# Output projection of a transformer block: the seventh product's weights are added onto the third's tiles in place

## The chip, the cores and the metric

One core of one Trainium2 chip runs the whole kernel. The metric is device time in microseconds of one execution; for each kernel it is the median of several runs. The profile is one execution recorded by the hardware profiler.

## What is computed

A block with adaptive layer norm, a mixer of a short convolution and sparse attention, an output projection and a gated FFN, on 512 tokens of width 2048, everything in float32. The change is in the output projection, whose place is:

```
y_conv = short_conv_mixer(cb, cc, ch, conv_w)          # 512 x 1024, then a norm
y_attn = nsa_mixer(q, kc, vc, ksl, vsl, kw, vw, gl..)  # 512 x 1024, then a norm
x = x + g_a * (concat([y_conv, y_attn]) @ w_out)       # w_out: 2048 x 2048
h = modulate(rms_norm(x, norm_ffn), sh_f, sc_f)
x = x + g_f * ((silu(h @ ffn_w1) * (h @ ffn_w3)) @ ffn_w2)
```

## The kernel before, in words

TensorE multiplies float32 matrices as three products of rounded parts: every operand is split into a high part (ScalarE casts it to fp32r, tiles `whi`) and a low part (VectorE subtracts the high part from the source, `wlo`).

The projection is cut into 2 x 2 x 2 blocks of 256 tokens, 1024 rows and 1024 columns of `w_out`, and is done with seven block products in place of eight (a Strassen-Winograd scheme). A product is named by its number p, in the order 2, 1, 5, 6 and 3 interleaved, 7, 4. Its weights are eight blocks j = 0 to 7 of 128 x 1024 floats (512 KB), so that (p, j) is one unit of work: a load or an addition of weights, a split of the block (`y_split`, L1216 to L1234), and twelve matmuls of 128 x 512 (`y_mm`, L1242). The 56 units are numbered in the list `yu`: product 2 is 0 to 7, product 1 is 8 to 15, product 5 is 16 to 23, products 6 and 3 share 24 to 39, product 7 is 40 to 47, product 4 is 48 to 55. Units 36 to 41 are (6,6), (6,7), (3,6), (3,7), (7,0) and (7,1). Of product 7 the last two units, of product 4 the last three are multiplied together.

The weights of products 1, 5, 6 and 4 lie in eight tiles `wt` and are made one out of the other: B11 is loaded, B12 added (product 5), B22 added (product 6), B21 added (product 4). Product 3's weights are B22 as it is, and VectorE adds the same tiles onto `wt` for product 6 (L1446). Product 7's weights are B12 + B22. Before the change B12 is loaded for them by SP (L1208) and B22 is then added onto it by a DMA that accumulates (`added`, L1180). Accumulating DMAs are issued by GpSimd (POOL in the profile), one after the other in the order in which the code names them.

The places of these blocks are the four `raw` tiles of a ring, for j = 4 and 5 a piece of `x2T`, and for some blocks the four tiles `H6` (6455 to 6458 in the order's rows), each of which holds half a block. `H6` holds the left operand of product 6 and comes free in product 6's first units.

In the loop over units (from L1485 on) step n first does what `steps_at` holds for it (loads, adds, sums), then splits unit n + 2, multiplies unit n, and then does what `behind` holds (the left operands' splits `y_form`, the sums of finished blocks, stores, transposes for the FFN). The results go, gated by `ga`, onto the residual: `first_block` (rows 0 to 255, columns 1024 to 2047, ready with products 2 and 1), `sixth` and `gated(1, 2, ...)` (the first half's other block, ready with product 3), `fifth` and the last ones (the second half). `x_store` writes a block to memory, `x_load` and `x22_load` bring the residual.

The order in which an engine gets its instructions is not that of the code: the framework arranges them by its own estimate of when each can run, except where `issue_after` pins one behind another. Each engine then works through its queue in order, so that an instruction that waits holds those behind it. Behind the projection the FFN begins; its first weights are loaded by SP into the `raw` ring (L1644), and split at L1569 and L1576.

Of the kernel before, what the change touches and what calls it, by code (L numbers as in the profile page):

```python
# [70 lines left out]
def block_kernel(ctx: ExitStack, tc: tile.TileContext, a: dict, out: bass.AP):  # L71
    nc = tc.nc
# [1100 lines left out]
    def ring_place():  # L1173
        return in_four(ring[0].tile([P, 1024], F32, tag="raw", name="raw"))

    added_last, loaded_last = [], [None]

    def added(to, src):
        with tc.issue_after(added_last[-1]) if added_last else ExitStack():
            added_last.append(nc.gpsimd.dma_start(to, src, accum_op=ALU.add).ins)  # L1180

    def y_load(p, j):
        if p == 2:
            WB[p, j] = ring_place()
            nc.sync.dma_start(WB[p, j], w_block(2, 1, j))
        elif p == 1:
            for q in (1, 5, 6, 4):
                WB[q, j] = in_four(WT[j])
            nc.sync.dma_start(WB[p, j], w_block(1, 1, j))
        elif p == 5 and j < 4:  # L1190
            WB["b", j] = ring_place()
            nc.sync.dma_start(WB["b", j], w_block(1, 2, j))
        elif p == 5:
            added(WB[p, j], w_block(1, 2, j))
        elif p == 3:
            WB[p, j] = x2T[:, 4 * j - 8:4 * j - 4, 0:HS] if j in (4, 5) else ring_place()
            nc.sync.dma_start(WB[p, j], w_block(2, 2, j))
        elif p == 7:
            if j < 2:
                to = WB[p, j] = YF["H6"][2 * j:2 * j + 2]  # L1200
            else:
                WB[p, j] = x2T[:, 4 * j - 8:4 * j - 4, 0:HS] if j in (4, 5) else ring_place()
                to = [WB[p, j]]
            for c in (1, 2):
                for n, t in enumerate(to):
                    src = w_block(c, 2, j)[:, 4 // len(to) * n:4 // len(to) * (n + 1)]
                    if c == 1:
                        loaded_last[-1] = nc.sync.dma_start(t, src).ins  # L1208
                    else:
                        added(t, src)  # L1210
        elif p == 4:
            added(WB[p, j], w_block(2, 1, j))

# [2 lines left out]
    def y_split(p, j):  # L1216
        if (p, j) == (7, 7):
            ts = [act1.tile([P, S], F32R, tag="ahi", name="w77") for _ in range(4)]
            hi, lo = ts[0:2], ts[2:4]
        else:  # L1220
            hi, lo = [[wtp[2 * j - 10 + h].tile([P, 1024], F32R, tag="wt", name="w4")] for h in range(2)] if p == 4 and j > 4 else \
                ([ring[1].tile([P, 1024], F32R, tag="hi", name="whi")], [ring[2].tile([P, 1024], F32R, tag="lo", name="wlo")])
        src, m = WB[p, j], len(hi)
        if isinstance(src, list):
            cuts = [[t[0][:, n * 512:(n + 1) * 512] for t in (hi, lo)] for n in range(2)]
            todo = [(h, l, s_) for (h, l), s_ in zip(cuts, src)]
        else:
            todo = [(h, l, src[:, 4 // m * n:4 // m * (n + 1)]) for n, (h, l) in enumerate(zip(hi, lo))]
        todo = [(h.rearrange("p (a b) -> p a b", b=HS), l.rearrange("p (a b) -> p a b", b=HS), s_) for h, l, s_ in todo]
        for h, l, s_ in todo:  # L1230
            nc.scalar.copy(h, s_)
        for h, l, s_ in todo:
            low_of[-1] = nc.vector.tensor_sub(l, s_, h.bitcast(F32)).ins
        y_hl[p, j] = [[t[n] if len(t) == 2 else t[0][:, n * 512:(n + 1) * 512] for n in range(2)] for t in (hi, lo)]  # L1234
# [84 lines left out]
    def x_of(r, c, t):  # L1319
        i = 2 * (r - 1) + t  # L1320
        return x[i * P:(i + 1) * P, (2 - c) * 1024:(3 - c) * 1024]

    def x_load(r, c):
        for t in range(2):
            if r == 2:
                twos["x", t] = t2p.tile([P, 1024], F32, tag="t2", name="x21")
                to = in_four(twos["x", t])
            else:
                k0 = (c - 1) * HK + 4 * t
                to = x2T[:, k0:k0 + 4, HS:S]  # L1330
            with tc.issue_after(loaded_last[-1]) if r == 2 else ExitStack():
                nc.sync.dma_start(to, x_of(r, c, t).rearrange("p (a b) -> p a b", a=4))

    def x22_load(t, n):
        nc.sync.dma_start(x2_of(2, 2, t, n), x_of(2, 2, t)[:, n * 512:(n + 1) * 512].rearrange("p (a b) -> p a b", a=2))

    def x_store(r, c, t):
        i = 2 * (r - 1) + t
        for n in range(2):
            to = xd[n][:, t, :] if (r, c) == (2, 2) else \  # L1340
                out[0, i * P:(i + 1) * P, (2 - c) * 1024 + n * 512:(2 - c) * 1024 + (n + 1) * 512]
            nc.gpsimd.dma_start(to.rearrange("p (a b) -> p a b", a=2), x2_of(r, c, t, n))

    tags = ["d1", "d2"] * 64

# [20 lines left out]
    def copies(bank):  # L1366
        for t in range(2):
            twos[bank, t] = t2p.tile([P, 1024], F32, tag="t2", name=f"c{bank}")
            for n in range(2):
                nc.scalar.copy(twos[bank, t][:, n * 512:(n + 1) * 512], ybank[bank][2 * t + n])  # L1370

    def first_block(t, n):
        u, x2 = two(), x2_of(1, 1, t, n)
        nc.vector.tensor_add(u, pair_of(ybank["x"][2 * t + n]), pair_of(twos["z", t][:, n * 512:(n + 1) * 512]))
        nc.vector.tensor_mul(u, u, gate_of(1, n))
        nc.vector.tensor_add(x2, x2, u)
        squared(1, 1, t, n, u)
# [62 lines left out]
    for j in range(HK):  # L1440
        at_unit(*yu[6 + j // 4 if j < 7 else 9], (y_load, 1, j))
        at_unit(*yu[6 + j if j < 4 else 7 + j], (y_load, 5, j))
        if j < 4:
            at_unit(*yu[12 + j], (w_sum, 5, j, "b"))
        at_unit(*yu[(13, 14, 15, 16, 17, 19, 25, 26)[j]], (y_load, 3, j))
        at_unit(*yu[yat[6, j] - 4], (lambda j: nc.vector.tensor_add(WB[6, j], WB[6, j], WB[3, j]), j))  # L1446
        at_unit(*yu[(24, 25, 28, 30, 32, 34, 37, 38)[j]], (y_load, 7, j))
        at_unit(*yu[(27, 31, 35, 39, 40, 41, 42, 43)[j]], (y_load, 4, j))
    for q in (2, 3, 0, 1):
        at_unit(2, 7, (lambda q: nc.gpsimd.dma_start(ga[:, q * 512:(q + 1) * 512], gad[q].to_broadcast([P, 512])), q))  # L1450
    at_unit(1, 2, (x_load, 1, 1))
    at_unit(1, 4, (x_load, 1, 2))
    for q in range(4):
        at_unit(*yu[24 + 2 * q], (x22_load, q // 2, q % 2))
    at_unit(7, 3, (x_load, 2, 1))
    behind = {}

    def behind_unit(p, j, *todo):
# [4 lines left out]
            behind_unit(*yu[n], (y_form, p, j))  # L1463
    behind_unit(2, 7, (copies, "z"))
    for q, (t, n) in enumerate(TN):
        behind_unit(5, (0, 1, 3, 4)[q], (first_block, t, n))
        behind_unit(*yu[(30, 32, 33, 35)[q]], (fifth, t, n))
        behind_unit(7, q, (gated, 1, 2, t, n, "y"))
    for t in range(2):
        behind_unit(6, 0, (x_store, 1, 1, t))  # L1470
        behind_unit(4, 2, (x_store, 1, 2, t))
        behind_unit(4, 1, (x_store, 2, 2, t))
    behind_unit(5, 7, (copies, "y"))
    behind_unit(6, 7, (sixth,))
# [159 lines left out]
    def plain_steps():  # L1634
        os = [{"b": {}} for _ in range(PLAIN)]
        h = [slice(0, HS), slice(HS, S)]
        three = []

        def make(u, q, w, j):
            o = os[u]  # L1640

            def load():
                t = o["b"][q] = ring[0].tile([P, HK * P], F32, tag="raw", name="raw")
                nc.sync.dma_start(t.rearrange("p (k n) -> p k n", k=HK), block(u, q))  # L1644
# [481 lines left out]
```

## Time and profile before

| | |
|---|---|
| Runs of the kernel | 2146.9, 2148.47, 2151.5 us (median 2148.47) |
| Profiled execution | 2148.66 us, span 2146.9 us, mean granted TensorE clock 0.998 |
| Busy in the span | PE 2117.9 us (99%), DVE 1773.1 (83%), ACT 1043.2 (49%), POOL 254.9 (12%) |
| Projection, 673 to 847 us of the span | TensorE busy 164.5 of 173.5 us, granted clock 0.98, DMA 0.82 busy at 224 GB/s |
| DMAs issued at 670 to 850 us | 40.10 MB moved, of it 16.10 MB on GpSimd's queue, 23.85 MB on SP's |

The rows of the trace that the prediction quotes are read so. In the order of time a row has the start in us from the span's start, the duration in us, the engine (PE matmul, PEld weight load, DVE VectorE, ACT ScalarE, POOL GpSimd, SP SyncE, with a q for the engine's queue of issues), the line of the kernel, the operation, output <- input, the shape, the count, and in brackets the idle time of that engine before it and what ended it. A row with two or more merged instructions has the time from the first's start to the last's end. In the DMA view a row has output <- input, the issuing queue, the count, the KB of each, and the median time in us from the issue to the landing. Matmuls overlap: one lasts 0.39 us in the rows while they start 0.23 us apart.

### The profile page before, as it was taken

Reading aid. Unit: us, or ns where it says so; the run is one execution under the profiler, and the core shown is the slowest. Engines: PE = TensorE matmul, PEld = TensorE weight load, DVE = VectorE, ACT = ScalarE, POOL = GpSimd, SP = SyncE. Lnnn points to the kernel's source line nnn. Section 1 sums busy time; section 2 is a strip of 40 time slices with the busy share of each in tenths; the row PEclk is TensorE's granted clock in tenths of the full one; section 3 lists DMA queues with packets and bytes.
Section 4 is the critical chain, followed back from the end, with each engine's and each line's share of the span. In section 5 each row is a group of like instructions: output and inputs, shape, how many; then the busy total and the mean of one; then the engine's idle time right before and its main releaser. Section 6 shows DMA issues by size and latency. Waiting matters only on the chain.

```text
span 2146.9 us, 30986 instructions
## 1 busy us (share of the span) xinstructions
PE 2117.9 (99%) x11453; PEld 1778.9 (83%) x11453; DVE 1773.1 (83%) x2596; ACT 1043.2 (49%) x1665; POOL 254.9 (12%) x326
## 2 busy tenths in 40 slices
PE   7999999999999989999999999999999999999999
PEld 6778778888888868888888888888888887888887
DVE  7788658888788977888888888888888887878788
ACT  5226244555555547644444444444444555444543
POOL 0000200000000220001111111111111122211110
PEclk9999999999999999999999999999999999999999
DMA  9985638756668984598878877888787599797975
GB/s 339 363 272 192 201 100 252 217 163 206 179 184 272 258 199 138 139 248 206 201 191 189 209 196 187 203 195 203 184 202 182 144 301 295 145 307 138 290 157 139
DMA packets 452234, 450.20 MB, mean 210 GB/s; under 512 B 20707, under 2 KB 379147, under 8 KB 451442
## 3 DMA queue, kind: packets, MB, share of 16 engines
q1 hardware_dynamic: 379678, 333.00, 50.2%
q0 software_dynamic: 71872, 114.74, 26.9%
q8 instruction: 90, 1.47, 0.3%
q10 hardware_dynamic: 532, 0.48, 0.1%
q14 instruction: 62, 0.51, 0.1%
HBM read 428.19 MB, written 19.96 MB: 209 GB/s over the span
## 4 chain that ended last, share of the span: by engine, by line
PE 89%; DVE 4%; DMA 4%; issue 1%; SPq 1%; ACT 1%; ACTq 0%; DVEq 0%; POOLq 0%
PE main L1582 15%; PE aux L1582 11%; PE aux L1981 9%; PE main L1981 9%; PE main L1588 8%; PE aux L1588 6%; PE main L121 5%; PE main L123 5%; PE main L122 5%; PE aux L1242 2%; PE aux L121 2%; PE aux L989 2%; PE aux L123 2%; PE aux L122 2%; DMA raw<-in_w_out 1%
## 5 line engine op out<-in xcount | busy, mean ns | idle before, releaser
L1569 ACT CAST whi<-raw 128x1024 fp32r<-128x1024 f32 x246 | 257.6, 1051 | 259.1 <-PE main L1582 122.1
L1582 PE MATMUL main<-hC,whi 128*128 128x512 f32 x1408 | 347.1, 392 | 0.3 <-ACT whi L1569 0.2
L1576 DVE TENSOR_TENSOR wlo<-raw,whi 128x1024 fp32r<-128x1024 f32 x218 | 266.1, 1221 | 86.1 <-PE aux L1588 42.0
L1569 ACT CAST whi<-t 128x1024 fp32r<-128x1024 f32 x186 | 195.5, 1051 | 248.1 <-PE main L1981 62.1
L1582 PEld LDWEIGHTS main<-hC,whi 128*128 128x128 f32 x1408 | 256.9, 188 | 53.1 <-DVE d L1601 2.7
L1582 PE MATMUL aux<-hC,whi 128*128 128x512 f32 x1072 | 264.4, 391 | 0.0
L1582 PEld LDWEIGHTS aux<-hC,whi 128*128 128x128 f32 x1072 | 196.3, 188 | 38.2 <-issue 0.6
L1588 PEld LDWEIGHTS main<-hC,wlo 128*128 128x128 f32 x1408 | 184.9, 191 | 7.8
L1588 PE MATMUL main<-hC,wlo 128*128 128x256 f32 x1408 | 191.2, 283 | 0.0
L121 PE MATMUL main<-alo,whi 128*128 128x512 f32 x432 | 174.2, 404 | 0.0
L123 PE MATMUL main<-ahi,whi 128*128 128x512 f32 x432 | 170.3, 395 | 0.0
L122 PE MATMUL main<-ahi,wlo 128*128 128x512 f32 x432 | 169.1, 391 | 0.0
L1588 PE MATMUL aux<-hC,wlo 128*128 128x256 f32 x1072 | 148.5, 282 | 0.0
L1953 DVE TENSOR_TENSOR wlo<-t,whi 128x1024 fp32r<-128x1024 f32 x102 | 124.2, 1220 | 29.1 <-ACT whi L1569 29.0
L1588 PEld LDWEIGHTS aux<-hC,wlo 128*128 128x128 f32 x1072 | 142.1, 191 | 6.4
L1576 DVE TENSOR_TENSOR wlo<-t,whi 128x1024 fp32r<-128x1024 f32 x84 | 102.6, 1221 | 37.3 <-issue 13.4
L1981 PE MATMUL main<-wlo,ghi 128*128 128x512 f32 x304 | 118.5, 390 | 1.4 <-DVE wlo L1953 1.2
L1981 PE MATMUL aux<-whi,glo 128*128 128x512 f32 x308 | 119.8, 389 | 0.0
L1981 PE MATMUL aux<-whi,ghi 128*128 128x512 f32 x308 | 119.8, 389 | 0.0
L1981 PE MATMUL aux<-wlo,ghi 128*128 128x512 f32 x308 | 119.7, 389 | 0.0
L1981 PE MATMUL main<-whi,ghi 128*128 128x512 f32 x304 | 118.3, 389 | 0.0
L1981 PE MATMUL main<-whi,glo 128*128 128x512 f32 x304 | 118.3, 389 | 0.0
(426 smaller groups left out, 4173.7 us busy)
## 6 DMA issues: line engine op xcount, KB each, us to landing
raw<-in_ffn_w SPq DMA_DIRECT2D x204, 512.0 KB, 5.7
t<-in_ffn_w POOLq DMA_DIRECT2D x90, 512.0 KB, 6.8
t<-in_ffn_w SPq DMA_DIRECT2D x78, 512.0 KB, 5.9
araw<-in_ada_w SPq DMA_DIRECT2D x56, 512.0 KB, 8.7
raw<-in_w_in SPq DMA_DIRECT2D x128, 192.0 KB, 4.0
raw<-in_w_in SPq DMA_DIRECT2D x38, 512.0 KB, 4.9
kT<-in_ada_w SPq DMA_DIRECT2D x35, 512.0 KB, 4.4
accs<-in_ada_w POOLq DMA_DIRECT2D x64, 256.0 KB, 4.9
```

The costliest lines, as they stand in the source:

```text
L121: nc.tensor.matmul(ps, lhs[0], rhs[1], start=first, stop=False)
L122: nc.tensor.matmul(ps, lhs[1], rhs[0], start=False, stop=False)
L123: return nc.tensor.matmul(ps, lhs[0], rhs[0], start=False, stop=last).ins
L989: nc.tensor.matmul(po[:, b * HD:(b + 1) * HD], s["pT"][b][:, kb * P:(kb + 1) * P], vv[b][:, kb, g * HD:(g + 1) * HD], start=kb == 0, stop= ...
L1242: nc.tensor.matmul(ps, l, w, start=m == 0 and j == 0 and p in (1, 5, 2), stop=m == 2 and j == HK - 1 and p in (3, 2, 4), skip_group_check= ...
L1569: hi_ins[-1] = nc.scalar.copy(hi, t).ins
L1576: lo_ins[-1] = nc.vector.tensor_sub(lo, t, hi.bitcast(F32)).ins
L1582: nc.tensor.matmul(ps, wt[0][:, k * P:(k + 1) * P], hc(p, k), start=first and k == 0, stop=False, skip_group_check=True)
L1588: nc.tensor.matmul(ps[:, HS:], wt[1][:, k * P:(k + 1) * P], hc(p, k)[:, 0:HS], start=False, stop=last and k == HK - 1, skip_group_check=True)
L1953: W["last"] = nc.vector.tensor_sub(lo, t, hi.bitcast(F32)).ins
L1981: nc.tensor.matmul(ps[2 * t + c], x_[:, j, tok], w[:, cs], start=m == 0 and j == 0 and p in (1, 5, 2), stop=m == 2 and j == GS[b] - 1 and ...
```

## The change

1. The third product's tiles become the seventh's. `y_load` loads B22 for (3, j) into a place that is kept (`WB[3, j] = WB[7, j]`), and for (7, j) only adds B12 onto it, in place, after (3, j) was split. The eight loads of B12 and the eight adds of B22 for product 7 go; eight adds of B12 come. (3,6) and (3,7) lie in `H6` now, in halves, and so does product 7 there, where before (7,0) and (7,1) lay in it. The loads of (3,6) and (3,7) are named at units 21 and 24 instead of 25 and 26, the adds for product 7 one unit ahead of (3, j).
2. The sum for product 6 (`second_sum`) takes the third product's block in pieces where it lies in two tiles.
3. `first_block` is cut: its first sum stays in product 5 (`first_sum`, units 16, 17, 19 and 20), the product with the gate, the sum onto the residual and the square go behind units 25, 27, 29 and 31; `fifth` goes from units 30, 32, 33, 35 to 33, 35, 38, 39.
4. Stores and loads: block (1,1) is stored by GpSimd behind unit 33 (before: unit 24), block (1,2) by SP at unit 44 (before: by GpSimd behind unit 50), the residual's load for the second half at unit 44 instead of 43, and the FFN's first loads are pinned behind that load.

The core of it (names of lists, and the same helper in `y_split`, are left out):

```diff
     def y_load(p, j):
...
         elif p == 3:
-            WB[p, j] = x2T[:, 4 * j - 8:4 * j - 4, 0:HS] if j in (4, 5) else ring_place()
-            nc.sync.dma_start(WB[p, j], w_block(2, 2, j))
+            to = [ring_place()] if j < 4 else [x2T[:, 4 * j - 8:4 * j - 4, 0:HS]] if j < 6 else YF["H6"][2 * j - 12:2 * j - 10]
+            WB[3, j] = WB[7, j] = to
+            for t, src in pieces(to, w_block(2, 2, j)):
+                asked_last.append(nc.sync.dma_start(t, src).ins)
         elif p == 7:
-            if j < 2:
-                to = WB[p, j] = YF["H6"][2 * j:2 * j + 2]
-            else:
-                WB[p, j] = x2T[:, 4 * j - 8:4 * j - 4, 0:HS] if j in (4, 5) else ring_place()
-                to = [WB[p, j]]
-            for c in (1, 2):
-                for n, t in enumerate(to):
-                    src = w_block(c, 2, j)[:, 4 // len(to) * n:4 // len(to) * (n + 1)]
-                    if c == 1:
-                        loaded_last[-1] = nc.sync.dma_start(t, src).ins
-                    else:
-                        added(t, src)
+            for t, src in pieces(WB[p, j], w_block(1, 2, j)):
+                added(t, src)
...
+    def second_sum(j):
+        for to, t in pieces(WB[3, j], WB[6, j]):
+            nc.vector.tensor_add(t, t, to)
...
+            if (r, c) == (1, 2):
+                asked(to, x2, True)
+            else:
+                with tc.issue_after(added_last[-1]) if (r, c) == (1, 1) else ExitStack():
+                    nc.gpsimd.dma_start(to, x2)
...
+    def first_sum(t, n):
+        u = block1[t, n] = two()
+        nc.vector.tensor_add(u, pair_of(ybank["x"][2 * t + n]), pair_of(twos["z", t][:, n * 512:(n + 1) * 512]))
+
     def first_block(t, n):
-        u, x2 = two(), x2_of(1, 1, t, n)
-        nc.vector.tensor_add(u, pair_of(ybank["x"][2 * t + n]), pair_of(twos["z", t][:, n * 512:(n + 1) * 512]))
+        u, x2 = block1[t, n], x2_of(1, 1, t, n)
...
-        at_unit(*yu[(24, 25, 28, 30, 32, 34, 37, 38)[j]], (y_load, 7, j))
+        at_unit(*yu[yat[3, j] - 1], (y_load, 7, j))
...
-    at_unit(7, 3, (x_load, 2, 1))
+    at_unit(7, 4, (x_store, 1, 2, 0), (x_store, 1, 2, 1), (x_load, 2, 1))
...
-                nc.sync.dma_start(t.rearrange("p (k n) -> p k n", k=HK), block(u, q))
+                with tc.issue_after(asked_last[-1]) if u == 0 else ExitStack():
+                    nc.sync.dma_start(t.rearrange("p (k n) -> p k n", k=HK), block(u, q))
```

What stands where in the engines' queues, at three places. First ScalarE around the beginning of product 7, before. `whi_7574` is (7,0), `whi_7596` (7,1), `whi_7618` (7,2), `whi_7642` (7,3); the two `w77` are the halves of (7,7), which lies in `raw_7571`; `form` are left operands.

```order
L1231 CAST whi_7574<-H6_6455 128x512
L1231 CAST whi_7574<-H6_6456 128x512
L1043 CAST form_7710<-E5_6365 128x256
L1231 CAST whi_7596<-H6_6457 128x512
L1231 CAST whi_7596<-H6_6458 128x512
L1043 CAST form_7733<-E5_6366 128x256
L1231 CAST whi_7618<-raw_7340 128x1024
L1043 CAST form_7764<-E5_6366 128x256
L1231 CAST w77_7744<-raw_7571 128x512
L1231 CAST w77_7745<-raw_7571 128x512
L1231 CAST whi_7642<-raw_7383 128x1024
```

The same place of ScalarE after. `whi_7527` is (3,7), `whi_7562` (7,0), `whi_7584` (7,1), `whi_7606` (7,2); (3,7) and (7,7) both lie in `H6_6457` and `H6_6458`.

```order
L1233 CAST whi_7527<-H6_6457 128x512
L1233 CAST whi_7527<-H6_6458 128x512
L1043 CAST form_7670<-E5_6365 128x256
L1233 CAST whi_7562<-raw_6977 128x1024
L1043 CAST form_7694<-E5_6365 128x256
L1233 CAST w77_7738<-H6_6457 128x512
L1233 CAST w77_7739<-H6_6458 128x512
L1233 CAST whi_7584<-raw_7000 128x1024
L1043 CAST form_7727<-E5_6366 128x256
L1233 CAST whi_7606<-raw_7023 128x1024
```

The casts of (7,7) stood between (7,2) and (7,3) and stand between (7,0) and (7,1) now, two units further ahead.

Second GpSimd's accumulating DMAs of the end of product 3 and of product 7, before: the `x2T` are (7,4) and (7,5), `raw_7537` and `raw_7571` are (7,6) and (7,7), the `wt` product 4's.

```order
L1180 DMA x2T_6773<-in_w_out 128x4x256 x2
L1180 DMA wt_6800<-in_w_out 128x1024
L1180 DMA raw_7537<-in_w_out 128x1024
L1180 DMA raw_7571<-in_w_out 128x1024
L1180 DMA wt_6801<-in_w_out 128x1024
```

After, with (7,6) and (7,7) in the four halves of `H6`:

```order
L1180 DMA x2T_6773<-in_w_out 128x4x256
L1352 DMA out_0<-x2T_6773 128x2x256 x4
L1180 DMA x2T_6773<-in_w_out 128x4x256
L1180 DMA wt_6800<-in_w_out 128x1024
L1180 DMA H6_6455<-in_w_out 128x512
L1180 DMA H6_6456<-in_w_out 128x512
L1180 DMA H6_6457<-in_w_out 128x512
L1180 DMA H6_6458<-in_w_out 128x512
L1180 DMA wt_6801<-in_w_out 128x1024
```

The adds of (7,6) and (7,7) keep their place among product 4's; the four stores of block (1,1) came in between (7,4) and (7,5).

Third SP's loads in product 5 and at the beginning of product 6, before: the `H6` are (7,0) and (7,1), `raw_7276` is (3,6), `raw_7298` (3,7), the `H3` the residual's.

```order
L1208 DMA H6_6455<-in_w_out 128x512
L1208 DMA H6_6456<-in_w_out 128x512
L1208 DMA H6_6457<-in_w_out 128x512
L1335 DMA H3_6692<-in_x 128x512
L1208 DMA H6_6458<-in_w_out 128x512
L1335 DMA H3_6693<-in_x 128x512
L1335 DMA H3_6694<-in_x 128x512
L1197 DMA raw_7276<-in_w_out 128x1024
L1335 DMA H3_6695<-in_x 128x512
L1197 DMA raw_7298<-in_w_out 128x1024
```

After, the four `H6` are (3,6) and (3,7):

```order
L1207 DMA H6_6455<-in_w_out 128x512
L1207 DMA H6_6456<-in_w_out 128x512
L1207 DMA H6_6457<-in_w_out 128x512
L1327 DMA H3_6692<-in_x 128x512
L1207 DMA H6_6458<-in_w_out 128x512
L1327 DMA H3_6693<-in_x 128x512
L1327 DMA H3_6694<-in_x 128x512
L1327 DMA H3_6695<-in_x 128x512
```

(3,6) moved from the eighth to the first two rows, (3,7) from the tenth to the third and fifth; the loads of product 7 are gone.

More of the change, by code (lines that the diff above doesn't have):

```diff
@@ L1174, in ring_place @@
         return in_four(ring[0].tile([P, 1024], F32, tag="raw", name="raw"))
-    added_last, loaded_last = [], [None]
+    added_last, asked_last = [], []
     def added(to, src):
@@ L1180, in added, with pieces @@
             added_last.append(nc.gpsimd.dma_start(to, src, accum_op=ALU.add).ins)
+    def pieces(to, src):
+        m = 4 // len(to)
+        return [(t, src[:, m * n:m * (n + 1)]) for n, t in enumerate(to)]
+    def second_sum(j):
+        for to, t in pieces(WB[3, j], WB[6, j]):
+            nc.vector.tensor_add(t, t, to)
     def y_load(p, j):
@@ L1222, in y_split @@
                 ([ring[1].tile([P, 1024], F32R, tag="hi", name="whi")], [ring[2].tile([P, 1024], F32R, tag="lo", name="wlo")])
[L1223 to L1226, printed above, removed]
-        else:
-            todo = [(h, l, src[:, 4 // m * n:4 // m * (n + 1)]) for n, (h, l) in enumerate(zip(hi, lo))]
+        src = WB[p, j] if isinstance(WB[p, j], list) else [WB[p, j]]
+        if len(hi) > len(src):
+            src = [t for _, t in pieces(hi, src[0])]
+        if len(hi) < len(src):
+            cuts = [[t[0][:, n * 512:(n + 1) * 512] for n in range(2)] for t in (hi, lo)]
+        else:
+            cuts = hi, lo
+        todo = list(zip(*cuts, src))
         todo = [(h.rearrange("p (a b) -> p a b", b=HS), l.rearrange("p (a b) -> p a b", b=HS), s_) for h, l, s_ in todo]
@@ L1321, in x_of, with asked @@
         return x[i * P:(i + 1) * P, (2 - c) * 1024:(3 - c) * 1024]
+    def asked(to, src, held):
+        with tc.issue_after(asked_last[-1]) if held else ExitStack():
+            asked_last.append(nc.sync.dma_start(to, src).ins)
     def x_load(r, c):
@@ L1330, in x_load @@
                 to = x2T[:, k0:k0 + 4, HS:S]
-            with tc.issue_after(loaded_last[-1]) if r == 2 else ExitStack():
-                nc.sync.dma_start(to, x_of(r, c, t).rearrange("p (a b) -> p a b", a=4))
+            asked(to, x_of(r, c, t).rearrange("p (a b) -> p a b", a=4), r == 2)
     def x22_load(t, n):
-        nc.sync.dma_start(x2_of(2, 2, t, n), x_of(2, 2, t)[:, n * 512:(n + 1) * 512].rearrange("p (a b) -> p a b", a=2))
+        asked(x2_of(2, 2, t, n), x_of(2, 2, t)[:, n * 512:(n + 1) * 512].rearrange("p (a b) -> p a b", a=2), False)
     def x_store(r, c, t):
@@ L1341, in x_store @@
                 out[0, i * P:(i + 1) * P, (2 - c) * 1024 + n * 512:(2 - c) * 1024 + (n + 1) * 512]
-            nc.gpsimd.dma_start(to.rearrange("p (a b) -> p a b", a=2), x2_of(r, c, t, n))
+            to, x2 = to.rearrange("p (a b) -> p a b", a=2), x2_of(r, c, t, n)
+            if (r, c) == (1, 2):
[3 more added lines that the diff above has]
+                    nc.gpsimd.dma_start(to, x2)
     tags = ["d1", "d2"] * 64
@@ L1370, in copies @@
                 nc.scalar.copy(twos[bank, t][:, n * 512:(n + 1) * 512], ybank[bank][2 * t + n])
+    block1 = {}
+    def first_sum(t, n):
+        u = block1[t, n] = two()
+        nc.vector.tensor_add(u, pair_of(ybank["x"][2 * t + n]), pair_of(twos["z", t][:, n * 512:(n + 1) * 512]))
     def first_block(t, n):
-        u, x2 = two(), x2_of(1, 1, t, n)
-        nc.vector.tensor_add(u, pair_of(ybank["x"][2 * t + n]), pair_of(twos["z", t][:, n * 512:(n + 1) * 512]))
+        u, x2 = block1[t, n], x2_of(1, 1, t, n)
         nc.vector.tensor_mul(u, u, gate_of(1, n))
@@ L1444, in block_kernel @@
             at_unit(*yu[12 + j], (w_sum, 5, j, "b"))
-        at_unit(*yu[(13, 14, 15, 16, 17, 19, 25, 26)[j]], (y_load, 3, j))
-        at_unit(*yu[yat[6, j] - 4], (lambda j: nc.vector.tensor_add(WB[6, j], WB[6, j], WB[3, j]), j))
-        at_unit(*yu[(24, 25, 28, 30, 32, 34, 37, 38)[j]], (y_load, 7, j))
-        at_unit(*yu[(27, 31, 35, 39, 40, 41, 42, 43)[j]], (y_load, 4, j))
+        at_unit(*yu[(13, 14, 15, 16, 17, 19, 21, 24)[j]], (y_load, 3, j))
+        at_unit(*yu[yat[6, j] - 4], (second_sum, j))
+        at_unit(*yu[yat[3, j] - 1], (y_load, 7, j))
+        at_unit(*yu[(28, 32, 36, 39, 40, 41, 42, 43)[j]], (y_load, 4, j))
     for q in (2, 3, 0, 1):
@@ L1465, in block_kernel @@
     for q, (t, n) in enumerate(TN):
-        behind_unit(5, (0, 1, 3, 4)[q], (first_block, t, n))
-        behind_unit(*yu[(30, 32, 33, 35)[q]], (fifth, t, n))
+        behind_unit(5, (0, 1, 3, 4)[q], (first_sum, t, n))
+        behind_unit(*yu[(25, 27, 29, 31)[q]], (first_block, t, n))
+        behind_unit(*yu[(33, 35, 38, 39)[q]], (fifth, t, n))
         behind_unit(7, q, (gated, 1, 2, t, n, "y"))
     for t in range(2):
-        behind_unit(6, 0, (x_store, 1, 1, t))
-        behind_unit(4, 2, (x_store, 1, 2, t))
+        behind_unit(*yu[33], (x_store, 1, 1, t))
         behind_unit(4, 1, (x_store, 2, 2, t))
```

## The prediction

> **What bounds the kernel now.** I read the span first, then the busy time in three stretches (before, during and behind the output projection), then TensorE's row in order of time through the projection. In the rows of stretches the columns are the stretch, its length, and the busy time of PE, PEld, DVE, ACT and POOL with their instructions, then granted clock, DMA share and GB/s.
>
> ```profile
> span 2146.9 us, 30986 instructions
> 673.30:846.80 173.50, 164.49 (x764) 136.29 (x763) 139.82 (x198) 101.78 (x183) 32.63 (x43) 0.98 0.82 224
> 846.80:2146.90 1300.10, 1293.08 (x6877) 1113.11 (x6875) 1089.59 (x1338) 628.23 (x795) 191.54 (x230) 1.00 0.80 201
> ```
>
> TensorE is the bound: behind the projection it is idle for 1300.10 - 1293.08 = 7.0 us in 1300, so whatever the projection saves reaches the end, microsecond for microsecond. The projection itself has 173.50 - 164.49 = 9.0 us of idle TensorE, at two places. The larger, in TensorE's row in order of time:
>
> ```profile
> 783.89 0.39 PE L1242 MATMUL aux<-wlo,form 128*128 128x512 f32 x1
> ...
> 791.60 0.61 PE L1242 MATMUL aux<-whi,form 128*128 128x512 f32 x2
> 800.54 0.80 PE L1242 MATMUL aux<-wlo,form 128*128 128x512 f32 x1 [8.33 <-DVE wlo L1233]
> ...
> 804.33 0.39 PE L1242 MATMUL aux<-wlo,form 128*128 128x512 f32 x1
> 804.56 0.61 PE L1242 MATMUL aux<-whi,form 128*128 128x512 f32 x2
> 805.01 0.39 PE L1242 MATMUL aux<-wlo,form 128*128 128x512 f32 x1
> ```
>
> 783.89 is the start of the seventh product. Three matmuls take 805.01 - 804.33 = 0.68 us, a unit of twelve 2.72 us. So (7,3) was due at 783.89 + 3 x 2.72 = 792.05 and started at 800.54. Its first nine matmuls then took 804.33 - 800.54 = 3.79 us where 2.04 are usual, because the clock was down:
>
> ```profile
> 797.50:800.50 3.00, 0.00 (x0) 0.00 (x0) 1.24 (x2) 3.00 (x6) 0.00 (x0) 0.50 1.06 213
> ```
>
> The stall costs 8.49 us of waiting and 1.75 us of slow matmuls (granted clock 0.50 in the last 3 us of the wait, and still down when the work resumes), **10.24 us**. What it waited for stands in ScalarE's, VectorE's and GpSimd's rows; the last row is the DMA view of GpSimd's issue at 783.89, with its size and the time to landing.
>
> ```profile
> 797.15 1.14 ACT L1231 CAST w<-raw 128x512 fp32r<-128x512 f32 x2 [11.70 <-DMA raw<-in_w_out]
> 798.19 1.04 ACT L1231 CAST whi<-raw 128x1024 fp32r<-128x1024 f32 x1
> ```
>
> ```profile
> 799.26 1.23 DVE L1233 TENSOR_TENSOR wlo<-raw,whi 128x1024 fp32r<-128x1024 f32 x1 [11.06 <-ACT whi L1231]
> ```
>
> ```profile
> 783.89 0.84 POOL L1180 DMA_DIRECT2D raw<-in_w_out  x1 [1.11 <-DVE wlo L1233]
> raw<-in_w_out POOLq DMA_DIRECT2D x1, 512.0 KB, 13.2
> ```
>
> ScalarE stood 11.70 us in front of the two casts of (7,7) (tile w), which are queued ahead of (7,3)'s cast. (7,3)'s own weights were not what was missing: its cast follows at once. (7,7)'s were, whose add was issued at 783.89 and landed 13.2 us later. The smaller stall:
>
> ```profile
> 752.50 0.61 PE L1242 MATMUL aux<-whi,form 128*128 128x512 f32 x2
> 753.80 0.50 PE L1242 MATMUL main<-wlo,form 128*128 128x512 f32 x1 [0.68 <-DVE wlo L1233]
> 754.14 0.64 PE L1242 MATMUL main<-whi,form 128*128 128x512 f32 x2
> 754.61 0.40 PE L1242 MATMUL main<-wlo,form 128*128 128x512 f32 x1
> ```
>
> ```profile
> 751.38 1.23 DVE L1446 TENSOR_TENSOR wt<-wt,raw 128x1024 f32<-128x1024 f32 x1 [1.90 <-DMA raw<-in_w_out]
> 743.55 0.33 SPq L1197 DMA_DIRECT2D raw<-in_w_out  x1
> ```
>
> The load of (3,6) was issued at 743.55; the sum that reads it (L1446) held VectorE's queue for 1.90 us, and (3,2)'s subtraction stood behind it. A group of three is one matmul with wlo and 0.23 us later two with whi (804.33 and 804.56). The last group of (6,2) has its pair at 752.50, so it began at 752.27, (3,2) was due at 752.95 and its second group at 753.63; that one began at 754.61: **0.98 us**. Both stalls together: 10.24 + 0.98 = 11.2 us.
>
> **The change part by part.** The profiled execution took 2148.66 us (span 2146.9 and 1.8 around it), 0.2 above the median of the three runs, 2148.47; the sum is made against 2148.66. With both stalls gone it is 2148.66 - 11.2 = 2137.4.
>
> *Loads of the third product.* (3,6) and (3,7) now take the places on SP at which the seventh product's first loads stood, so (3,6) is asked for by 722, 20 us earlier, and the sum finds it there:
>
> ```profile
> 711.24 10.72 SPq L1208 DMA_DIRECT2D H<-in_w_out  x3
> ```
>
> The 0.98 us go whole; nothing else in that stretch was late by a DMA.
>
> *Eight loads of the seventh product are gone* (8 x 512 KB), and its adds need no load in front. By the POOL rows of the order six of the eight blocks are added long before their product begins. The last two lie in H6, where an add may start when the third product's own split has read the block. So what is late next is (7,7) again: its two casts now stand between (7,0)'s and (7,1)'s. I put time 0 at the start of unit (6,7), 775.73 in the profile before, three units ahead of (7,0) at 8.16 and four ahead of (7,1) at 10.88. The rows are those of the same steps before (TensorE, ScalarE, VectorE, one after the other), and from the DMA view the landings of the quarter-megabyte adds into H6, of the first ones and of the last of three that were queued one behind the other:
>
> ```profile
> 775.73 0.39 PE L1242 MATMUL aux<-wlo,form 128*128 128x512 f32 x1
> 778.65 1.14 ACT L1231 CAST whi<-H 128x512 fp32r<-128x512 f32 x2 [1.36 <-PE aux L1242]
> 778.35 1.88 DVE L1426 TENSOR_TENSOR d<-aux,ga 128x512 f32<-128x512 f32 x3
> 780.15 2.49 DVE L1429 TENSOR_TENSOR x2T<-x2T,d 128x512 f32<-128x512 f32 x4
> 782.56 2.49 DVE L1233 TENSOR_TENSOR wlo<-H,whi 128x512 fp32r<-128x512 f32 x4
> H<-in_w_out POOLq DMA_DIRECT2D x2, 256.0 KB, 4.4
> H<-in_w_out POOLq DMA_DIRECT2D x1, 256.0 KB, 6.2
> ```
>
> A block's casts begin 0.20 us after the unit two ahead of it (778.65, where that unit began at 775.73 + 2.72 = 778.45). So (3,7)'s, now two halves, end at 0.20 + 1.14 = 1.34, the second half's subtraction (2.49 / 4 = 0.62) at 2.0. Then the add of (7,7)'s second half can be issued. It lands 4.4 to 6.2 us later, at 6.4 to 8.2; behind it come one cast of (7,7) (1.14 / 2 = 0.57), (7,1)'s cast (1.05) and subtraction (1.23), 2.9 with the hand-over. (7,1) is ready at 9.3 to 11.1, and due at 10.88: a wait of nothing to 0.2 us. (7,0) has a margin as thin: VectorE is free of (3,7) at 2.0 and then does four products (0.60 each), four sums (782.56 - 780.15 = 2.41) and (7,0)'s subtraction, now one of 1.23 where two halves stood, and ends at 8.0 against 8.16. I take **0.3 us** for the two together. The granted clock stays up, as it did over the 0.68 us wait at 753.80 (no matmul there took over 0.50).
>
> [...]
>
> *The first block's tail moves* from the fifth product (units 16 to 20) to units 25 to 31: eight VectorE operations of 0.6 us. VectorE's busy time before, and its margin at (3,0), the first unit that the moved work could make late:
>
> ```profile
> 720.00:740.00 20.00, 20.00 (x90) 16.57 (x89) 20.00 (x28) 13.87 (x26) 5.55 (x7) 1.00 0.84 237
> 742.32 1.21 DVE L1233 TENSOR_TENSOR wlo<-raw,whi 128x1024 fp32r<-128x1024 f32 x1
> 744.80 0.39 PE L1242 MATMUL main<-wlo,form 128*128 128x512 f32 x1
> ```
>
> VectorE has no idle time there, so it does the same operations in another order and reaches (3,0) no later: its subtraction ended at 742.32 + 1.21 = 743.53, and the margin is 744.80 - 743.53 = 1.27 us. Nothing is charged. The block's four stores now stand on GpSimd between the adds of (7,4) and (7,5), some 0.8 us of issue each. Behind them (7,6)'s and (7,7)'s adds wait for the splits of (3,6) and (3,7), which come 4 units and more later, 10.9 us against 3.2: nothing is charged here either.
>
> *SP.* The first half's second block is stored from SP, and the residual's and the FFN's first loads stand behind these four stores, which wait for VectorE's gated sums of units 40 to 43. Nothing else is queued there.
>
> ```profile
> 786.43 53.68 SPq L1644 DMA_DIRECT2D raw<-in_ffn_w  x7
> 830.17 1.09 ACT L1569 CAST whi<-raw 128x1024 fp32r<-128x1024 f32 x1
> ```
>
> The FFN's first load was issued at 786.43 and first read at 830.17, 44 us. It moves behind unit 43, which now ends at 783.89 - 0.98 + 4 x 2.72 = 793.8, to about 795 with the issues in front of it, and the reading to 830.17 - 11.2 = 819: 24 us are left, where the longest landing quoted below is 21.1. Charged: nothing; if this cover failed, each us would cost one.
>
> The sum: 2148.66 - 10.24 - 0.98 + 0.3 = **2137.7 us**.
>
> **The rivals.** *Starved adds.* Behind time 2.0 VectorE runs without a gap until 8.0, and GpSimd's issues into H6 fall in that run. If they got through only behind it, the add would land at 8.0 + 4.4 = 12.4, (7,1) would be ready at 15.3, a wait of 4.4 us with 1.75 of slow clock: 2137.4 + 6.2 = 2143.6. Against it:
>
> ```profile
> 755.00:760.00 5.00, 5.00 (x24) 4.11 (x23) 5.00 (x8) 1.75 (x3) 0.84 (x1) 1.00 0.42 113
> 757.62 0.84 POOL L1180 DMA_DIRECT2D raw<-in_w_out  x1 [14.12 <-DVE wt L1446]
> raw<-in_w_out POOLq DMA_DIRECT2D x1, 512.0 KB, 5.2
> ```
>
> An issue in five microseconds of full VectorE took 0.84 us, and its add landed after 5.2. Chance 0.10. [...]
>
> *The same wait in another place* (the change does not do what it says). (7,7) lands as late behind its split as before, 13.2 us: ready at 2.0 + 13.2 + 2.9 = 18.1, a wait of 7.2 and 1.75 of slow clock, 2146.4, within 0.2% of before. For it: the casts stand even further ahead. Against it: the 13.2 were spent behind two other adds and two loads. Chance 0.06.
>
> *Slower.* The queue is as full as it was for the next adds:
>
> ```profile
> wt<-in_w_out POOLq DMA_DIRECT2D x1, 512.0 KB, 21.1
> ```
>
> With 21.1 us (7,1) is ready at 26.0, waits 15.1 and loses 1.75: 2154.3. The wait exceeds what is saved when the landing takes over 15.5 us (2.0 + 15.5 + 2.9 - 10.88 + 1.75 = 11.3). Against it: on GpSimd the adds that landed so late now stand behind (7,7)'s. Chance 0.06.
>
> *VectorE becomes the bound.* If the moved 8 x 0.6 = 4.8 us do not fill gaps but add up, (3,0) is 4.8 - 1.27 = 3.5 us late: 2141.2. Chance 0.06.
>
> **How the numbers follow.** The forecast keeps 0.72. A change of 0.2%, 4.3 us, is about what a measurement of this kernel can tell from none. Faster by more: the forecast, the starved adds and VectorE, 0.88; within: 0.06; slower: 0.06. The forecast's own range is 2135.5 to 2139.5, about half the spread of the runs before (2146.9 to 2151.5) to each side. The low end stays; upwards the range takes in VectorE and the starved adds, to 2144.0, and leaves out 0.12.
>
> **What would show it.** Right: no TensorE idle at 752; (3,6)'s sum without a DMA wait; ScalarE's wait at (7,7)'s casts no longer than 6 us; TensorE's wait at (7,1) under 1 us and the clock at 1.00 to the end of the stage; the projection's end near 836, where the third stretch begins at 846.8 now. Wrong: a wait of (7,1) for VectorE over 3 us, an add into H6 that lands after more than 8 us, a wait at (3,0), or ScalarE waiting for the FFN's first load.

## The result and the profile after

The changed kernel took 2138.03 us in the median of four runs (2137.41 to 2138.62), beside 2148.59 for the kernel before: a ratio of 0.9949, 95% interval 0.9932 to 0.9967, 10.6 us faster. The prediction was 2137.7. The profiled execution took 2138.62 us, its span 2136.8. One run each of e6_late40 and after_again, and one of the kernel before beside the latter, took 2621 to 4265 us and are left out of all ratios below.

First the span and two rows of stretches of the changed kernel, cut at 835.60, 1.9 us before the projection's last matmul ends at 837.49 (stretch, length, busy time of PE, PEld, DVE, ACT, POOL, then clock, DMA share and GB/s):

```profile
span 2136.8 us, 30970 instructions
...
673.30:835.60 162.30, 161.29 (x759) 133.94 (x758) 138.62 (x198) 101.00 (x182) 29.24 (x38) 1.00 0.80 211
835.60:2136.80 1301.20, 1294.84 (x6885) 1114.54 (x6883) 1091.21 (x1343) 628.99 (x797) 191.42 (x231) 1.00 0.80 201
```

TensorE's idle time in the projection fell from 9.0 us to 162.30 - 161.29 = 1.0, and the clock stays at 1.00. In the second stretch TensorE is idle for 1301.20 - 1294.84 = 6.4 us, where it was 7.0. All of the 1.0 us is one wait, in the list of TensorE's waits from 673.30 to 860 us:

```profile
PE aux L1244 <- DVE wlo L1235: 1.0, 1, 1.0
```

The list held 8.3 us for `aux` and 0.7 us for `main` before. TensorE's row in order of time shows both old places and the new one:

```profile
752.72 0.39 PE L1244 MATMUL aux<-wlo,form 128*128 128x512 f32 x1
752.94 0.62 PE L1244 MATMUL aux<-whi,form 128*128 128x512 f32 x2
753.39 0.39 PE L1244 MATMUL main<-wlo,form 128*128 128x512 f32 x1
...
783.31 0.48 PE L1244 MATMUL aux<-wlo,form 128*128 128x512 f32 x1
...
785.48 0.39 PE L1244 MATMUL aux<-wlo,form 128*128 128x512 f32 x1
785.70 0.61 PE L1244 MATMUL aux<-whi,form 128*128 128x512 f32 x2
787.33 0.50 PE L1244 MATMUL aux<-wlo,form 128*128 128x512 f32 x1 [1.01 <-DVE wlo L1235]
```

(3,2) follows (6,2) at 753.39, 0.67 us behind the group at 752.72: no stall. (7,0) starts at 783.31. (7,1) was due 2.72 us later, at 786.03, and started at 787.33, 1.30 late: (7,0) itself ran 0.13 us longer than usual (its last group began at 785.48, 0.68 us before 786.16), and the rest is the wait ahead of (7,1). ScalarE's row at that place, and from the DMA view the landings of GpSimd's issues of 778.0 to 778.6, tell why:

```profile
783.18 0.62 ACT L1233 CAST w<-H 128x512 fp32r<-128x512 f32 x1 [3.75 <-DMA H<-in_w_out]
784.45 0.62 ACT L1233 CAST w<-H 128x512 fp32r<-128x512 f32 x1 [0.65 <-DMA H<-in_w_out]
784.97 1.04 ACT L1233 CAST whi<-raw 128x1024 fp32r<-128x1024 f32 x1
```

```profile
H<-in_w_out POOLq DMA_DIRECT2D x1, 256.0 KB, 6.8
```

The casts of (7,7) (tile `w`) still hold ScalarE's queue, for 3.75 + 0.65 = 4.4 us where it was 11.70, and (7,1)'s cast still follows at once. The add of the second half landed 6.8 us after its issue.

### The profile page after: what moved, and what is told of

The parts are those of the page before. It is cut to its first block, busy times and chain, and to the rows that moved or that the text cites. A ratio compares the mean times of both kernels' runs of the same rounds, so it can differ in the third digit from the quotient of the medians.

```text
span 2136.8 us, 30970 instructions
## 1 busy us (share of the span) xinstructions
PE 2116.0 (99%) x11453; PEld 1777.6 (83%) x11453; DVE 1773.0 (83%) x2599; ACT 1042.7 (49%) x1666; POOL 251.3 (12%) x322
## 3 DMA queue, kind: packets, MB, share of 16 engines
HBM read 424.00 MB, written 19.96 MB: 208 GB/s over the span
## 4 chain that ended last, share of the span: by engine, by line
PE 93%; DMA 2%; DVE 2%; issue 1%; SPq 1%; ACT 1%; POOL 0%; ACTq 0%; DVEq 0%; POOLq 0%
PE main L1597 15%; PE aux L1597 11%; PE aux L1997 10%; PE main L1997 9%; PE main L1603 8%; PE aux L1603 6%; PE main L121 6%; PE main L123 5%; PE main L122 5%; PE aux L1244 4%; PE main L1244 3%; PE aux L121 2%; PE aux L989 2%; PE aux L123 2%; PE aux L122 2%; PE aux L980 1%
```

## The experiments

The theory (T1): the gain is the time for which ScalarE's queue was held by casts that stood at its head and waited for a late add of (7,7), 10.24 us, and 0.98 us of VectorE held by the load of (3,6). The rivals: T2, the 4 MB of loads that are gone; T3, the moved tail and stores of the first block. Each kernel was timed in five runs (e1_tail_in_before in eleven) beside the kernel before on the same chip: e1, e2, e3 and e6_late40 on one chip, e2b, e4_twice_sbuf, e7 and e6b on a second, the last three on a third. Between chips only the ratios are compared.

**The moved tail alone, in the kernel before (e1_tail_in_before).** Part 3 of the change, and of part 4 only the later store of block (1,1):

```diff
-        behind_unit(5, (0, 1, 3, 4)[q], (first_block, t, n))
-        behind_unit(*yu[(30, 32, 33, 35)[q]], (fifth, t, n))
+        behind_unit(5, (0, 1, 3, 4)[q], (first_sum, t, n))
+        behind_unit(*yu[(25, 27, 29, 31)[q]], (first_block, t, n))
+        behind_unit(*yu[(33, 35, 38, 39)[q]], (fifth, t, n))
...
-        behind_unit(6, 0, (x_store, 1, 1, t))
+        behind_unit(*yu[33], (x_store, 1, 1, t))
```

> The kernel before with only the first block's tail cut in two (its sum stays in the fifth product, the gate, the second sum and the square go to units 25, 27, 29, 31), the fifth product's tail to units 33, 35, 38, 39, and the store of the first block to unit 33; the seventh product's weights are still loaded and added apart. T1 (the gain is ScalarE's wait for the add of (7,7), 10.2 us, and DVE's wait for the load of (3,6), 1.0 us): both waits stay, 2147.5 to 2149.5 us, and the wait of about 8.5 us before unit (7,3) is still in the list of waits. T3 (the gain comes from the moved tail and stores): 2138 to 2143.

Measured: 2147.31 us against 2149.01 for the kernel before, ratio 0.9991 (0.9983 to 1.0). TensorE's waits in the projection:

```profile
PE aux L1242 <- DVE wlo L1233: 8.3, 1, 8.3
```

The large wait is there in full, so T3 does not hold it. The small one, at (3,2), is gone from this profile: the sum that waits for the load of (3,6) began 5.5 us after the load's issue here (748.17 behind 742.71), 7.8 us in the kernel before (751.38 behind 743.55). That may be the 1.7 us; the interval just reaches 1, and what hastened the load was not tried.

**Only the order in ScalarE's queue, in the kernel before (e2_pin_in_before).** One pin in the split:

```diff
         for h, l, s_ in todo:
-            nc.scalar.copy(h, s_)
+            with tc.issue_after(cast_of[7, 5]) if (p, j) == (7, 7) else ExitStack():
+                cast_of[p, j] = nc.scalar.copy(h, s_).ins
```

In the order of the five engines' queues four rows differ from the kernel before, all on ScalarE: the two casts of (7,7) out of one place and into another.

> The kernel before with one thing changed: ScalarE's two casts of (7,7) stand behind the cast of (7,5) instead of ahead of that of (7,3). No transfer, no sum and no matmul is changed or moved, and the 4 MB of loads that the change removes are still made. T1: ScalarE is no longer held by the add of (7,7), the wait of 8.49 and the slow clock of 1.75 behind it go: 2148.5 - 10.2 = 2138.3, between 2138 and 2140 us, and the wait of 1.0 us at unit (3,2) stays. T2 (the gain is the 4 MB less traffic): 2148 to 2149. T3 (the moved tail): 2148 to 2149.

Measured: 2141.05 us, ratio 0.996 (0.9947 to 0.9972). T2 and T3 expected 2148; the order alone brought 8 us. But it is 2 us short of T1. TensorE's waits in its profile, then ScalarE's row:

```profile
PE aux L1243 <- DVE d L1362: 2.0, 2, 1.3
PE main L1243 <- DVE wlo L1234: 1.8, 1, 1.8
PE aux L1243 <- DVE wlo L1234: 0.2, 1, 0.2
```

```profile
799.43 1.14 ACT L1232 CAST w<-raw 128x512 fp32r<-128x512 f32 x2 [3.17 <-DMA raw<-in_w_out]
...
807.87 1.05 ACT L1232 CAST w<-wt 128x1024 fp32r<-128x1024 f32 x1 [4.40 <-DMA wt<-in_w_out]
808.82 1.04 ACT L1232 CAST whi<-wt 128x1024 fp32r<-128x1024 f32 x1
```

The wait for the load of (3,6) was longer in this execution, the slowest of the five (1.8 us where it was 0.7, and 1.6 lost behind it with the granted clock at 0.53 from 755.40 to 758.80). And the next late add came into view: the first cast of (4,5) (tile `w` from `wt`) stands ahead of (4,1)'s in the queue and held it for 4.40 us; TensorE waited 2.0 us on VectorE's sums behind it. In the kernel before, no such wait is listed behind the large stall, which would cover it. The add of (7,7) was as late here as before (ScalarE's cast of it began at 799.43, where it was 797.15), and TensorE did not wait for it. The wait for (4,5) is, by the rows, the same mechanism one step on, which the next kernel tries.

**Two pins (e2b_two_pins).** As above, and the first cast of (4,5) behind that of (4,2):

```diff
+            last = {(7, 7): (7, 5), (4, 5): (4, 2)}.get((p, j))
+            with tc.issue_after(cast_of[last]) if last else ExitStack():
+                cast_of[p, j] = nc.scalar.copy(h, s_).ins
```

> The kernel before with ScalarE's casts of (7,7) behind the cast of (7,5), and besides the first cast of (4,5) behind that of (4,2) instead of ahead of that of (4,1). All transfers are those of before. T1: e2_pin_in_before came out at 2141.05, 2.3 over what was expected, because the next cast that stands in ScalarE's queue ahead of its turn, that of (4,5), waited 4.40 us for its own add and TensorE then lost 2.0 us in two waits at the start of the fourth product; with that cast behind (4,2) those go too: 2141.05 - 2.0 = 2139, between 2137.5 and 2140 us. What stays is the wait for the load of (3,6), 1 to 3.6 us with its slow clock. T2 (the rest is the 4 MB of traffic) and T3 (the rest is the moved tail): no further gain, 2141.

Measured: 2137.59 us against 2149.82, ratio 0.9946 (0.9934 to 0.9959), which is the changed kernel's gain. What is left of TensorE's waits in the projection:

```profile
PE main L1244 <- DVE wlo L1235: 0.6, 1, 0.6
```

No load is saved here, no tail of the first block is moved, no weight is added in place; the queues of GpSimd, SP and TensorE are those of before, row for row. The second pin moves more than its own row, though: in and behind the fourth product the framework also put eight other rows of ScalarE and seven of VectorE in another place. So the last 3 us are the order's, but not shown to be the one cast's. T2 and T3 as causes of the gain fall, and T1 stands, with one term more: the wait of (4,5), which the change removes as well (ScalarE waits there for no transfer), as GpSimd issues the fourth product's last five adds at 778.14 to 783.05 us there, and at 786.68 to 793.09 in e2_pin_in_before, behind the seventh product's loads and adds.

**The traffic put back (e4_twice_sbuf).** The changed kernel, (7,7)'s casts pinned as in e2_pin_in_before, and eight loads of 512 KB into 8 KB a partition of spare memory that nothing reads:

```diff
+        at_unit(*yu[(24, 25, 28, 30, 32, 34, 37, 38)[j]], (again, j))
...
+    def again(j):
+        with tc.issue_after(asked_last[-1]):
+            asked_last.append(nc.sync.dma_start(in_four(more[:, j % 2]), w_block(1, 2, j)).ins)
```

> The changed kernel with ScalarE's casts of (7,7) behind that of (7,5), as in e3_pin_in_after, and besides the 4 MB of loads that the change took away put back, at the units where the kernel before asks for them, into 8 KB a partition of otherwise unused memory that nothing reads. T2 (the gain is the traffic): the gain goes, 2146 to 2149. T1: the adds land later behind the loads, but no cast that stands at the head of a queue waits for one for long: 2136.7 to 2139.5.

Measured: 2137.24 us, ratio 0.9942 (0.993 to 0.9954). It reads as much from memory as the kernel before, 428.19 MB, where the changed one reads 424.00:

```profile
HBM read 428.19 MB, written 19.96 MB: 210 GB/s over the span
```

The last add of (7,7) landed after 8.3 us; without these loads it was 6.8 in the changed kernel's first profile, and 7.8 and 8.0 in after_again and e3_again below, so that the loads are not shown to have made it later. TensorE's list of waits in the projection is empty. T2 is refuted from this side too. (SP issued these loads at 721 to 759 us, ahead of the adds of (7,7), so that they met other adds than the loads of the kernel before did; that order was left as it was in e2b_two_pins.)

**The tail put back (e7_tail_back).** The changed kernel with the first block's gate, second sum and square behind units 16, 17, 19 and 20:

```diff
-        behind_unit(5, (0, 1, 3, 4)[q], (first_sum, t, n))
-        behind_unit(*yu[(25, 27, 29, 31)[q]], (first_block, t, n))
+        behind_unit(5, (0, 1, 3, 4)[q], (first_sum, t, n), (first_block, t, n))
```

> The changed kernel with the first block's tail (gate, second sum, square) back behind units 16, 17, 19 and 20 in the fifth product, as before; the fifth product's tail and the stores stay where the change put them. T3 (the moved tail carries part of the gain): 2141 or more. T1: the tail's 2.3 us of VectorE for each of four pieces is hidden in either place, 2137.4 to 2139.0, no measurable difference to the changed kernel.

Measured: 2137.57 us, ratio 0.9948 (0.9934 to 0.9961). In the changed kernel the tail's place is worth nothing that can be measured, as it was charged.

**A later add, in two places of the queue (e6_late40, e6b_late40_pin).** The adds of (7,7) behind two of the fourth product's; the second kernel has the pin behind (7,5) besides:

```diff
-        at_unit(*yu[yat[3, j] - 1], (y_load, 7, j))
+        at_unit(*yu[yat[3, j] - 1 if j < 7 else 40], (y_load, 7, j))
```

> The changed kernel with the two adds of (7,7) issued behind two of the fourth product's adds on GpSimd; the order's planner then puts ScalarE's casts of (7,7) ahead of the cast of (7,2) instead of (7,1). T1: the adds are issued about 2 us later and land behind 1 MB more, 9 to 13 us after their issue, at 788 to 792 on the profile's clock; unit (7,2), due at 788.75, is ready 2.9 us later, 791 to 795: it waits 2 to 6 us, and 0 to 1.75 more of slow clock, while the 1.3 us at (7,1) go: 2139 to 2144. T2 (only the traffic counts) and T3 (only the tail counts): 2138.0.

> e6_late40 (the two adds of (7,7) behind two of the fourth product's) with one thing changed: ScalarE's casts of (7,7) behind the cast of (7,5). The add lands as late as there. T1 (a late add costs only through the place of the casts that wait for it): the wait of 3.28 us before (7,2) and the 6.8 us of half clock behind it go, 2143.3 - 6.6 = 2136.7, between 2136 and 2138 us. Rival (a late add costs by itself, by the traffic it pushes back): 2141 to 2143.

Measured without the pin: 2139.98, 2140.18, 2143.33 and 2144.03 us, ratio 0.9964 (0.9951 to 0.9978); the profile is that of 2143.33. With the pin: 2137.68, ratio 0.9946 (0.9933 to 0.9958). The adds landed equally late in both, by the DMA view of the issues at 777.2 to 777.9 us, first without the pin, then with it:

```profile
wt<-in_w_out POOLq DMA_DIRECT2D x2, 512.0 KB, 14.7
H<-in_w_out POOLq DMA_DIRECT2D x2, 256.0 KB, 11.5
```

```profile
H<-in_w_out POOLq DMA_DIRECT2D x2, 256.0 KB, 12.0
```

Without the pin ScalarE and TensorE went so, each in its row in order of time:

```profile
787.27 0.62 ACT L1233 CAST w<-H 128x512 fp32r<-128x512 f32 x1 [6.00 <-DMA H<-in_w_out]
```

```profile
787.54 0.61 PE L1244 MATMUL aux<-whi,form 128*128 128x512 f32 x2
791.43 0.79 PE L1244 MATMUL aux<-wlo,form 128*128 128x512 f32 x1 [3.28 <-DVE wlo L1235]
...
797.67 0.39 PE L1244 MATMUL aux<-wlo,form 128*128 128x512 f32 x1
```

A group's pair of `whi` starts 0.23 us behind its `wlo`, so the last group of (7,1) began at 787.31 and (7,2) was due at 787.99. It started at 791.43, 3.44 us late; the five groups up to 797.67 then took 6.24 us instead of 3.40, 2.84 more, with the granted clock at 0.50 up to 797.20. With the pin TensorE's list of waits in the projection is empty. So in this execution the late add cost 3.44 + 2.84 = 6.3 us at the head of the queue. Two of the four runs lost less: by the ratios the mean cost is about 4 us, and the intervals of the two kernels, which ran on different chips, just overlap. Behind the pin an equally late add cost TensorE no wait, and the time is that of the changed kernel: the rival, that lateness costs by itself and gives 2141 to 2143, falls.

**The rest of the wait (e3_pin_in_after, e3_again, after_again).** The changed kernel with (7,7)'s casts behind (7,5)'s (the pin of e2_pin_in_before), and the changed kernel again beside it:

> The changed kernel with ScalarE's two casts of (7,7) behind the cast of (7,5) instead of ahead of that of (7,1). T1: what is left of the wait, 1.3 us at unit (7,1), is ScalarE's wait for the add of (7,7), so it goes: 2138.0 - 1.3 = 2136.7, between 2136.2 and 2137.4 us, with no wait of TensorE listed in the output projection. Rival (unit (7,1) is late because of VectorE or of the add of (7,1) itself): 2138.0.

> The changed kernel once more, to stand beside e3_again and e4c_twice_no_pin on one chip: 2137 to 2139 us, with the wait of 1.0 us before (7,1).

> e3_pin_in_after once more beside the changed kernel. T1: 1.0 to 1.3 us less than after_again, as the wait before (7,1) goes; 2136 to 2137.5. Rival (that wait is made up for later): within 0.4 us of after_again.

Measured: e3_pin_in_after 2136.73 us, ratio 0.9945 (0.9931 to 0.9958); on another chip e3_again 2137.6, ratio 0.9943 (0.9929 to 0.9957), beside after_again at 2137.8, ratio 0.9946 (0.9932 to 0.996). Both profiles with the pin show no TensorE wait in the projection. The wait itself is thus explained; it is no constant either, 2.04 us in after_again, where 1.0 was expected. But the kernels' times are not separated: the expected 1.0 to 1.3 us came out as 0.2, which is what the rival expected (that the wait is made up for later) and also less than one kernel's runs differ by. Which of the two it is stays open, and it is no proven improvement on the change.

**Traffic and the old place together (e4c_twice_no_pin).** e4_twice_sbuf without its pin, on the same chip as the last two.

> e4_twice_sbuf without the pin: the changed kernel in its own order of ScalarE's queue, with the 4 MB of loads put back into memory that nothing reads. With the pin those loads cost nothing (2137.24). T1: the add of (7,7) lands 8.4 us after its issue instead of 6.8, and the cast that waits for it stands again ahead of that of (7,1): the wait there grows from 1.0 to 2.6 to 3.5 us, and a wait of over 1.8 us has been followed by half clock that cost 1.6 to 3.4 us: 2140 to 2144. Rival (the loads are hidden in any order): within 1 us of after_again.

Measured: 2139.09 us, ratio 0.995 (0.9937 to 0.9963), 1.3 us above after_again, with this row in TensorE's order of time:

```profile
787.83 0.50 PE L1244 MATMUL aux<-wlo,form 128*128 128x512 f32 x1 [1.94 <-DVE wlo L1235]
```

The wait is longer than the 1.01 us of the changed kernel's first profile, but not than the 2.04 us of after_again beside it, and the last add landed 7.9 us after its issue, where it was 7.8 there. So the loads did not make the add later on this chip, against what the theory expected, and no half clock followed (1.00 in every stretch from 787 to 793). The time lies between the two expectations and the intervals overlap: the 1.3 us have no cause shown. What the run does show is that the gain stays with all the traffic back and no pin.

## Why the prediction was right

**The large stall (10.24 us): right.** It is gone from the trace, and e2b_two_pins shows the cause by itself: with the order of the queues as the only edit, the gain is the same. The change goes another way. It leaves the casts of (7,7) at the head of ScalarE's queue, even two units further ahead, but its add lands at 784.4 instead of 797.1: the second half is issued at 777.60 instead of 783.89, and lands 6.8 us later instead of 13.2. GpSimd's rows there, first before, then after:

```profile
779.73 1.27 POOL L1180 DMA_DIRECT2D x2T<-in_w_out  x1 [8.68 <-DMA x2T<-in_w_out]
```

```profile
777.00 1.70 POOL L1180 DMA_DIRECT2D H<-in_w_out  x2 [1.03 <-DVE wlo L1235]
```

Before, GpSimd stood 8.68 us for the load of (7,5), with the adds of (7,6) and (7,7) behind it; now no add there waits for a load. How much each part of this is worth was not separated.

The prediction did not see that the cast of (4,5) stood next in line. That the change takes this wait away too, as the fourth product's adds come up earlier behind adds that wait for no load, was luck: e2_pin_in_before, which removes the first wait alone, gained 8 us.

**The small stall (0.98 us): right in place, loose in size.** It is gone, as the load of (3,6) is issued at 710.67 instead of 743.55. Its size is not a constant of the kernel before: TensorE's wait there was 0.7 us in the profile before, 0.6 and 1.8 in two other executions with the same transfers, and nil in e1_tail_in_before.

**What is late next: right in place and cause, too small.** The forecast took 0.3 us for (7,0) and (7,1) together; it was 1.30, of it 0.13 within (7,0). (7,0)'s subtraction ended 0.07 us before its due time, as worked out (8.0 against 8.16). On the prediction's clock (time 0 at 775.15) the second half's add was issued at 2.5 instead of 2.0, since the first half's issue stands in front of it and the subtraction ended at 2.2, and landed at 9.3 instead of 6.4 to 8.2: the landing of 6.8 us was longer than the two rows it was taken from, 4.4 and 6.2. It was the last of four such adds in a row, where the 6.2 was the last of three; that this is the reason was not tried. In after_again it took 7.8, the wait was 2.04, and the clock, which the prediction had up to the end of the stage, was at 0.50 for about 3.4 us behind it. The prediction's own sign, a wait under 1 us at (7,1), was missed by little here (1.01) and clearly there.

**Charged nothing: right.** The tail (e7_tail_back); the stores; the FFN's first loads, issued at 798.79 instead of the expected 795 and first read at 821.33, 22.5 us of cover. The change also names the adds of (4,0) to (4,2) one unit later than before, which the prediction does not price; no run isolates it, and TensorE's list shows no wait there. **The rivals.** VectorE did not become the bound: (3,0) had no wait. GpSimd was not starved by VectorE's run: the two issues for (7,7), in the middle of it, took 1.70 us together, and the second half's add landed at 9.3 on the prediction's clock, where that rival had 12.4. No add of (7,7) in the changed kernel came near the 13.2 us of the other rivals; it took 11.5 and 12.0 us where e6_late40 and e6b_late40_pin moved it behind two others.

**The sum.** From the start of unit 24 to the last matmul of the projection the kernel before needed 846.86 - 739.36 = 107.50 us, the changed one 837.49 - 739.79 = 97.70: 9.8 less, where 11.22 - 1.30 = 9.9 are accounted for. The profiled execution, 2138.62 us, lies 0.9 above the forecast, near the 1.0 by which the last term was short; that the median, 2138.03, lies only 0.3 above it is the spread of the runs, and luck. The part ahead of unit 24 was 0.43 us longer and the FFN 0.7 shorter, which no part of the change explains; such differences occur between executions of one kernel (unit 24 began at 738.70 in after_again).

These rows begin and end that count, first of the kernel before, then of the changed one, TensorE in order of time (a row of several matmuls ends at its start plus its duration):

```profile
739.36 0.39 PE L1242 MATMUL aux<-wlo,form 128*128 128x512 f32 x1
...
838.44 8.42 PE L1242 MATMUL aux<-w,form 128*128 128x512 f32 x36
```

```profile
739.79 0.39 PE L1244 MATMUL aux<-wlo,form 128*128 128x512 f32 x1
...
829.06 8.43 PE L1244 MATMUL aux<-w,form 128*128 128x512 f32 x36
```

## What to carry to other kernels

When an engine waits long, look at what stands behind the waiting instruction in its queue: if that was ready, the cost is one of order, and a pin of a line or two may be worth as much as less traffic or less work (here the two pins gave a ratio of 0.9946, the change 0.9949). With the largest such wait gone, the next late transfer came into view here (4.40 us at (4,5)'s cast), so list all casts that stand ahead of their turn, and when their transfers land, before summing up a gain. And where several accumulating transfers are issued in a row, price the last one by a row of such a last one (6.8 us here, where the first of the four took 4.9).

## What the runs showed of the hardware

**A short wait cost as much by the half clock behind it as a long one.** A stretch of e6_late40 (clock third from the right) and a part of TensorE's row of after_again:

```profile
790.40:797.20 6.80, 5.77 (x14) 4.50 (x15) 6.80 (x10) 3.56 (x8) 0.00 (x0) 0.50 0.90 210
```

```profile
787.22 0.50 PE L1244 MATMUL aux<-wlo,form 128*128 128x512 f32 x1 [2.04 <-DVE wlo L1235]
787.56 0.99 PE L1244 MATMUL aux<-whi,form 128*128 128x512 f32 x2
788.34 0.63 PE L1244 MATMUL aux<-wlo,form 128*128 128x512 f32 x1
788.77 1.05 PE L1244 MATMUL aux<-whi,form 128*128 128x512 f32 x2
789.62 0.63 PE L1244 MATMUL aux<-wlo,form 128*128 128x512 f32 x1
```

With a wait of 3.28 us (e6_late40, to 791.43) came 6.8 us at 0.50, of which TensorE was at work for 5.8 and lost 2.84; in the kernel before the wait of 8.33 us, to 800.54, held about half of its own 6.8 us of slow clock (0.51 from 797.2 to 804.1), which cost only 1.75 in matmuls. After 2.04 us (the second fence: groups of 1.28 us where 0.68 is usual; clock 0.81 from 787 to 788, 0.50 from 788.0 to 791.0) and after 1.83 in e2_pin_in_before (0.53 from 755.40 to 758.80, 0.91 up to 760) there were about 3.4 us of slow clock, 1.7 and 1.6 us lost; after 1.94 in e4c_twice_no_pin (1.00 from 787 to 793) and after 1.0 in the changed kernel (1.00 from 786 to 792) none. Of the three waits of about 2 us two were followed by slow clock, then; why 1.94 us cost nothing where 1.83 cost 1.6 is not shown.

**The adds of a row landed one after the other.** The four of 256 KB that end the seventh product in the changed kernel are issued two and two from 774.28 to 778.70; the first landed after 4.9 us, at 779.2, the first of the second pair after 6.2, at 783.2, the last after 6.8, at 784.4. With two of 512 KB between them (e6_late40, e6b_late40_pin) the last pair took 11.5 us without the pin and 12.0 with it. VectorE worked without a gap from 776.0 to 783.2, and the pair of issues that fell within this took 1.70 us, the pair ahead of it 1.69.
